# Attention scores by two full 128-row passes in a hybrid SSD / differential attention / HGRN2 trunk

## The chip, the cores and the metric

One core of a Trainium2 chip runs the whole kernel. The metric is the device time of one execution in microseconds (us). TensorE (PE, with its weight loads shown apart as PEld), VectorE (DVE), ScalarE (ACT), GpSimd (POOL) and SyncE (SP) each work through their own list of instructions in order and wait for one another by semaphores. DMAs are issued from the SP, ACT and POOL queues.

## What is computed

Two residual layers on 1024 tokens of 1024 channels, then an RMSNorm. The part at issue is the differential attention of layer 0: 8 heads, each with two softmax maps of 64 channels.

```python
s = jnp.einsum("bqhcd,bkhcd->bhcqk", qi, k).astype(jnp.float32) * scale + bias[None, :, None]
s = jnp.where(rel >= 0, s, -jnp.inf)
p = jax.nn.softmax(s, axis=-1)
w = p[:, :, 0] - lam * p[:, :, 1]
return jnp.einsum("bhqk,bkhv->bqhv", w.astype(v.dtype), v)
```

The index c is the map (2), d the 64 channels of a map. Queries are taken in 8 row tiles of 128 tokens; row tile i needs (i + 1) * 128 keys.

## The kernel before

All products are made from float32r operands. Where more precision is wanted, an operand is held as a high part (its rounding) and a low part (the rest), and a product is the sum of high x high, high x low and low x high. Weights come in blocks of 256 columns (`_wprep`, L100 to L119: DMA, cast on ACT at L116, subtraction on DVE at L117), projections with channels on the partitions are made by `mm_cm` (L158, 24 passes of 512 tokens into one PSUM bank `pj`), those with tokens on the partitions by `mm_tm` (L168, passes of 256 columns).

Layer 0 does the four SSD groups first and then, for each of the 8 attention heads, `att_qk` (projects q and k of both maps), in most heads a projection of values or gates, and `att_core`. In `att_core`, `soft(i)` makes the scores of row tile i for map 0 and map 1 (L545, into one of the two `big` banks each), adds the bias and takes the row maximum (DVE L549, L553), exponentiates (ACT L559) and combines the maps (DVE L566). `values(i)` transposes the weights (PE L577, ACT L579) and multiplies them by V (PE L581). `norm` and its `tail` finish four row tiles (POOL L132, PE L600, DVE L627).

`att_qk` makes five tiles of 128 partitions x 1024 tokens per head, all from the pool tag "A" with 11 slots. Two are q's, one per map m: the 64 rows of the map hold the high part of q / 8, the other 64 its low part. `kh` holds the high parts of k of both maps below each other (ACT L519). Two are `kbs`: k's low part on the rows of the map (DVE L521) and k's high part on the other rows, which a DMA from the POOL queue brings from `kh` (L524, 64 rows x 1024, twice per head). A score is then a sum of two passes: q (128 rows) with `kbs` (128 rows), which gives both mixed products, and q's high rows with `kh`'s rows of that map (64 rows), which gives high x high.

The order of instructions on each engine is set by the Tile scheduler, which moves work of the next head and its projections between the steps of the present one; a slot of a pool is reused when its last reader is done, and what is to be written there waits for that reader.

Of the kernel before, what the change touches and what calls it, by code (L numbers as in the profile page):

```python
# [10 lines left out]
F32 = mybir.dt.float32  # L11
F32R = mybir.dt.float32r
# [21 lines left out]
def host_consts():  # L34
    c = {}
    c["ident"] = np.eye(P, dtype=np.float32)
    c["triu"] = np.triu(np.ones((P, P), np.float32))
    m = np.arange(384)
    rel = 255 - m
    n = np.maximum(rel, 0)  # L40
    large = 16 + (np.log(np.maximum(n, 1).astype(np.float32) / np.float32(16))
                  / np.float32(math.log(8.0)) * np.float32(16)).astype(np.int32)
    bucket = np.where(n < 16, n, np.minimum(large, 31))
    oh = np.zeros((33, 384), np.float32)
    oh[bucket, m] = (rel >= 0).astype(np.float32)
    oh[32] = np.where(rel < 0, NEG, 0.0)
    c["onehot"] = oh
    # HGRN2: keys (rows, modulo 32) that a query column of a region takes its weight from
    s = (np.arange(P) % 32)[:, None]
    reg = []  # L50
    for h, lo, hi in ((1, 0, 1), (2, 0, 2), (4, 2, 4), (4, 0, 2), (8, 0, 8), (16, 8, 16), (16, 0, 8)):
        seg, j = np.meshgrid(np.arange(16 // h), np.arange(h), indexing="ij")
        t = (seg * 2 * h + h + j).reshape(1, -1)
        o = s % (2 * h)
        reg.append(np.tile((s // (2 * h) == t // (2 * h)) & (o >= lo) & (o < hi), (1, NT)))
    c["lvmask"] = np.concatenate(reg, axis=1).astype(np.float32)
    c["dgmask"] = np.tile(s == np.arange(32)[None, :], (1, NT)).astype(np.float32)
    return c


SLOTS = {  # tag: (bytes per partition, slots); tiles of all phases share them
# [12 lines left out]
class Net:  # L74
# [22 lines left out]
    # weights: 256-column blocks, split exactly into two float32r parts  # L97
# [40 lines left out]
    # one 128-channel tile of u^T for four token tiles, times the norm's weight, split  # L138
# [10 lines left out]
    # channel-major product: [128 channels, 512 tokens]  # L149
# [12 lines left out]
    # token-major product: [128 tokens, 256 channels]  # L162
# [8 lines left out]
    # values, token-major, for two heads: two tiles of four token tiles  # L171
# [15 lines left out]
    # 2 silu(channel-major product), two tiles of 128 channels  # L187
# [21 lines left out]
def setup_rows(S):  # L209
# [5 lines left out]
    # per-channel vectors: rows of 128, turned into columns  # L215
# [29 lines left out]
def setup_rest(S):  # L245
# [10 lines left out]
    # HGRN2 lower bound of layer 1: softmax over the layers, its running sum less the first  # L256
# [21 lines left out]
    # lambda of the differential attention, on every partition  # L278
# [13 lines left out]
    # position bias: far value per head; near values in every row, read back skewed as Toeplitz tiles  # L292
# [15 lines left out]
def softplus(S, out, x, ax, e, s, s2):  # L308
    """max(x,0) + log1p(exp(-|x|)), log1p(e) = 2 atanh(e / (2 + e))"""
# [16 lines left out]
def dt_stage(S, u):  # L326
    """dt and the running sums of dt * A, tokens on the partitions: [128, chunk, head]"""
# [90 lines left out]
def ssd_core(S, g, xs, Bt, Ct, zg, ya):  # L418
# [4 lines left out]
    for c in range(NT):  # L423
# [44 lines left out]
        if c % 2 == 1:  # L468
            c2 = slice((c - 1) * P, (c + 1) * P)
            # exp(a_cs) along the rows, two heads per block  # L470
# [26 lines left out]
def att_qk(S, u):  # L497
    """q / 8 and k in two float32r parts: per map q's stacked, k's stacked the other way round (the mixed
    products in one pass), and both maps' high parts of k below each other"""
    nc = S.nc  # L500
    w = S.wnext()
    rows = slice(0, 64), slice(64, 128)
    qs = [S.t("A", [P, L], F32R) for _ in range(2)]
    for hf in range(2):
        sl = slice(hf * 512, hf * 512 + 512)
        pj = S.ps("pj")
        S.mm_cm(pj, w, 0, u, hf)
        for m in range(2):
            q, src = qs[m], pj[rows[m]]
            nc.scalar.activation(q[rows[m], sl], src, AF.Copy, scale=0.125)  # L510
            nc.vector.scalar_tensor_tensor(q[rows[1 - m], sl], src, 0.125, q[rows[m], sl].bitcast(F32),
                                           op0=ALU.mult, op1=ALU.subtract)
    kh = S.t("A", [P, L], F32R)
    kbs = [S.t("A", [P, L], F32R) for _ in range(2)]
    for hf in range(2):
        sl = slice(hf * 512, hf * 512 + 512)
        pj = S.ps("pj")
        S.mm_cm(pj, w, 1, u, hf)
        nc.scalar.copy(kh[:, sl], pj)  # L519
        for m in range(2):  # L520
            nc.vector.tensor_tensor(kbs[m][rows[m], sl], pj[rows[m]], kh[rows[m], sl].bitcast(F32),  # L521
                                    op=ALU.subtract)
    for m in range(2):
        nc.gpsimd.dma_start(kbs[m][rows[1 - m]], kh[rows[m]])  # L524
    return [(qs[m], kbs[m], qs[m][rows[m]], kh[rows[m]]) for m in range(2)]


def att_core(S, h, qk, V, sg, yb, tail):
    """tail: the last rows of the head before; returns its own"""
# [4 lines left out]
    def soft(i):  # L534
# [3 lines left out]
        for m in range(2):  # L538
            s = S.ps("big")
            f = max(n - 256, 0)  # L540
            for k0 in range(0, n, 512):
                kn = min(512, n - k0)
                for j in range(2):
                    q, k = qk[m][2 * j:2 * j + 2]
                    nc.tensor.matmul(s[:, k0:k0 + kn], lhsT=q[:, isl], rhs=k[:, k0:k0 + kn],  # L545
                                     start=(j == 0), stop=(j == 1))
# [76 lines left out]
def emit_y(S, pt, wcol, gate, dst):  # L623
    """(o^T * w) * gate for 512 tokens, stored"""
    nc = S.nc
    y = S.t("ey", [P, 512])
    nc.vector.scalar_tensor_tensor(y, pt, wcol, gate, op0=ALU.mult, op1=ALU.mult)  # L627
    nc.sync.dma_start(dst, y)


def load_y(S, y_d, wcols, hf, k, tags):
    """channel tiles k, k + 1, ... of y^T for 512 tokens, split: [hi | lo]"""
# [19 lines left out]
def out_proj(S, y_d, wcols, x_d, x1_tags, rs_a, finish):  # L652
    """x + y @ w_out in two parts: the channels that are there early for all tokens, which fills the wait
    for the others, then the others for 512 tokens at a time; finish(half, x1, 1 / rms)"""
# [41 lines left out]
    for hf in range(2):  # L696
        started = hf == 0
        if started:
            # all but the last channels, which come late: one open sum per bank
# [7 lines left out]
        for cb in range(4):  # L707
            # the last sums token tile by token tile, each in a bank of its own
# [61 lines left out]
def norm_first(S, x, wcol):  # L770
    """u of x in DRAM"""
# [54 lines left out]
def layer0(S, x, x1_d, u1):  # L826
# [14 lines left out]
    # 1 / rms of the gated rows (they carry a factor of two)  # L841
# [19 lines left out]
def layer1(S, x1_d, u, out):  # L861
# [50 lines left out]
    def early(cb, x1):  # L912
        # the norm's weight ahead of the row's scale; the squares are read before
        if cb < 3:
            nc.vector.tensor_tensor(x1, x1, bc(fws[cb].unsqueeze(1), list(x1.shape)), op=ALU.mult)
# [19 lines left out]
def hgrn_core(S, hd, g1, f, K, V, g2, att, lvm, dgm, yo):  # L935
    """Pairs (key, query) are split by the smallest block of 2h tokens that holds both; queries carry the
    decay from a boundary between the two, keys the decay up to it. One stationary key variant serves a
    level and the next one, whose queries come twice: for the far keys with the missing decay on top."""
# [69 lines left out]
    # keys of 32 and of 64 tokens; the former's weights on the partitions that the latter leaves  # L1008
# [14 lines left out]
    # the chunk's weights, keys on the partitions  # L1023
# [15 lines left out]
    # states  # L1039
# [80 lines left out]
```

## Time and profile before

| what | value |
|---|---|
| three runs | 2345.0, 2345.65 (median), 2347.86 us |
| profiled execution: span | 2346.1 us, 40804 instructions |
| PE busy | 2262.1 us (96%), 16868 matmuls |
| PEld / DVE / ACT / POOL busy | 1927.1 (82%) / 1269.5 (54%) / 824.8 (35%) / 187.5 us (8%) |
| chain that ended last | PE 83%, DMA 10%, DVE 4%, ACT 2%, issue 1% |
| L545 in it (`big`, the scores) | 5% |
| attention scores | L545, x384, first at 508.6 us, last at 1112.8 us |
| DMA issues of L524 | x16, 256 KB each, 5.5 us median from issue to landing |

The page gives no time for the profiled execution other than its span of 2346.1 us; that is 0.45 us over the median of the three runs. PE is the busy engine, but matmuls are pipelined and the profile models their ends, so the sum of their durations overstates them: the time that a matmul takes from PE is read as the distance from its start to the next one's start. The sentence "issue" behind an idle time means that the engine waited for nothing that the profile shows.

### The profile page before, as it was taken

What the parts mean: (1) busy time and instruction counts of PE and PEld (TensorE: products, weight loads), DVE (VectorE), ACT (ScalarE), POOL (GpSimd) and SP (SyncE); (2) the same over time, 40 slices, a digit from 0 to 9 for tenths busy, and PEclk for the clock granted to TensorE, in tenths of its full rate; (3) what the DMA queues carried; (4) which work ended last, traced back from release to release, by engine and by line L of the source; (5) the groups of instructions that cost most, each with busy time, mean ns of one, the idle gap of its engine ahead of it and who ended that gap; (6) DMA issues with size and microseconds to landing.
All of it is one profiled execution on the core that took longest, in us unless ns stands there. A gap on an engine that the chain in (4) does not pass through costs nothing.

```text
span 2346.1 us, 40804 instructions
## 1 busy us (share of the span) xinstructions
PE 2262.1 (96%) x16868; PEld 1927.1 (82%) x16868; DVE 1269.5 (54%) x2838; ACT 824.8 (35%) x1887; POOL 187.5 (8%) x201
## 2 busy tenths in 40 slices
PE   6959989899999999999999999999999999999998
PEld 4747766788778787788998888888888888989998
DVE  4736657535554545665444355555646465557444
ACT  4413333224444444544343223332323232334233
POOL 1000111100000000000001010101011010100000
PEclk9979999999999999999999999999999999999999
DMA  5342323231211211231432111111111111124323
GB/s 131 63 78 69 94 73 85 60 82 37 50 46 36 50 39 52 82 128 37 156 123 85 37 55 54 47 46 46 46 46 46 46 50 42 55 65 153 123 94 126
DMA packets 180701, 166.29 MB, mean 71 GB/s; under 512 B 9431, under 2 KB 162401, under 8 KB 180516
## 3 DMA queue, kind: packets, MB, share of 16 engines
q1 hardware_dynamic: 173668, 152.42, 21.5%
q0 software_dynamic: 2624, 7.08, 2.0%
q10 hardware_dynamic: 4224, 4.19, 0.5%
q8 instruction: 132, 2.16, 0.4%
q14 instruction: 53, 0.43, 0.1%
HBM read 132.66 MB, written 26.80 MB: 68 GB/s over the span
## 4 chain that ended last, share of the span: by engine, by line
PE 83%; DMA 10%; DVE 4%; ACT 2%; issue 1%; SPq 0%; POOL 0%; ACTq 0%; POOLq 0%; DVEq 0%
PE pj L158 38%; PE pj L168 21%; DMA G<-acs_d 6%; PE big L545 5%; PE big L168 5%; PE s L581 3%; PE big L976 2%; DMA tz_d<-o 1%; PE s L577 1%; PE big L1064 1%; PE big L1066 1%; PE s L1053 1%; DVE G L442 1%; PE big L1018 1%; DVE w_lo L117 1%
## 5 line engine op out<-in xcount | busy, mean ns | idle before, releaser
L158 PE MATMUL pj<-u,w_hi 128*128 128x512 f32 x3072 | 988.4, 399 | 12.2 <-ACT A L397 8.5
L158 PEld LDWEIGHTS pj<-u,w_hi 128*128 128x128 f32 x3072 | 570.4, 189 | 136.5 <-ACT A L397 9.7
L158 PE MATMUL pj<-u,w_lo 128*128 128x512 f32 x1536 | 609.7, 397 | 0.0
L168 PE MATMUL pj<-w_hi,u 128*128 128x256 f32 x2592 | 496.5, 287 | 1.0 <-DVE A L206 1.0
L168 PEld LDWEIGHTS pj<-w_hi,u 128*128 128x128 f32 x2592 | 409.6, 191 | 9.5 <-issue 5.6
L168 PE MATMUL pj<-w_lo,u 128*128 128x256 f32 x1296 | 370.2, 286 | 0.0
L158 PEld LDWEIGHTS pj<-u,w_lo 128*128 128x128 f32 x1536 | 290.2, 189 | 61.4 <-issue 2.2
L117 DVE TENSOR_TENSOR w_lo<-w_raw,w_hi 128x1024 fp32r<-128x1024 f32 x168 | 204.6, 1240 | 104.4 <-ACT w_hi L116 104.2
L168 PEld LDWEIGHTS pj<-w_lo,u 128*128 128x128 f32 x1296 | 248.0, 191 | 1.7 <-issue 0.6
L116 ACT CAST w_hi<-w_raw 128x1024 fp32r<-128x1024 f32 x168 | 168.0, 1046 | 200.2 <-PE pj L158 113.7
L545 PE MATMUL big<-A 128*128 128x512 f32 (+7 forms) x384 | 142.0, 420 | 0.0
L206 DVE SCALAR_TENSOR_TENSOR A<-th,pj 128x512 f32<-128x512 f32 x80 | 55.0, 688 | 143.9 <-ACT th L205 143.3
L205 ACT ACTIVATE th<-pj 128x512 f32<-128x512 f32 x96 | 57.2, 596 | 207.5 <-PE pj L158 202.7
L559 ACT ACTIVATE p<-p,mx 128x256 f32<-128x256 f32 (+7 forms) x128 | 98.7, 772 | 84.2 <-DVE mx L555 76.4
L545 PEld LDWEIGHTS big<-A 128*128 128x128 f32 (+1 forms) x384 | 71.2, 185 | 58.9 <-issue 50.6
L132 POOL TENSOR_TENSOR ro<-rs_t,mhalf 128x4 f32<-128x4 f32 x48 | 53.2, 1109 | 828.3 <-DVE rs_t L131 663.3
L579 ACT COPY wT<-s 128x512 f32<-128x512 f32 (+2 forms) x96 | 45.9, 478 | 134.4 <-PE s L577 133.9
L442 DVE TENSOR_SCALAR G<-G,ph 128x128 f32<-128x128 f32 x128 | 28.9, 287 | 108.1 <-DMA G<-acs_d 108.1
L893 POOL TENSOR_SCALAR A<-th,fN,fB 128x512 f32<-128x512 f32 x32 | 47.6, 1488 | 470.0 <-ACT th L890 470.0
L581 PE MATMUL s<-V,wT 128*128 128x128 f32 x576 | 81.2, 277 | 0.0
L960 DVE TENSOR_TENSOR A<-A,p 128x512 f32<-128x512 f32 x96 | 65.7, 685 | 23.5 <-PE big L976 23.0
L581 PEld LDWEIGHTS s<-V,wT 128*128 128x128 f32 x576 | 73.8, 191 | 4.5 <-issue 1.6
(328 smaller groups left out, 3030.7 us busy)
## 6 DMA issues: line engine op xcount, KB each, us to landing
w_raw<-in_even_w_in SPq DMA_DIRECT2D x32, 512.0 KB, 4.7
w_raw<-in_odd_w_in SPq DMA_DIRECT2D x64, 256.0 KB, 3.5
w_raw<-in_odd_w_in SPq DMA_DIRECT2D x32, 512.0 KB, 3.9
w_raw<-in_even_w_in SPq DMA_DIRECT2D x48, 256.0 KB, 3.9
w_raw<-in_even_w_out SPq DMA_DIRECT2D x24, 512.0 KB, 4.4
w_raw<-in_odd_w_out SPq DMA_DIRECT2D x24, 512.0 KB, 5.2
G<-acs_d SPq DMA_DIRECT2D x32, 256.0 KB, 4.7
yo<-ey SPq DMA_DIRECT2D x32, 256.0 KB, 2.0
```

What stands on the lines that cost most here:

```text
L116: nc.scalar.copy(hq, raw)
L117: nc.vector.tensor_tensor(lq, raw, hq.bitcast(F32), op=ALU.subtract)
L132: nc.gpsimd.tensor_tensor(dst, t[:, :n], self.mhalf[:, :n], op=ALU.pow)
L158: nc.tensor.matmul(out, lhsT=ww[:, k, ms], rhs=uu[k][:, sl], start=(n == 0), stop=(n == 3 * KT - 1))
L168: nc.tensor.matmul(out, lhsT=uu[k], rhs=ww[:, k, :], start=(k == 0 and j == 0), stop=(k == KT - 1 and j == 2))
L205: nc.scalar.activation(th, pj, AF.Tanh, scale=0.5)
L206: nc.vector.scalar_tensor_tensor(out, view(th), 1.0, view(pj), op0=ALU.add, op1=ALU.mult)
L442: nc.vector.tensor_scalar(R[:, h], R[:, h], S.acs[:, c, 4 * g + h:4 * g + h + 1], 0.0, op0=ALU.subtract, op1=ALU.min)
L545: nc.tensor.matmul(s[:, k0:k0 + kn], lhsT=q[:, isl], rhs=k[:, k0:k0 + kn], start=(j == 0), stop=(j == 1))
L559: nc.scalar.activation(p[:, :n], p[:, :n], AF.Exp, bias=mx, accum_out=z)
L581: nc.tensor.matmul(po[:, i % 4, :], lhsT=wT[:, j * P:j * P + P], rhs=V(j, hh), start=(j == 0), stop=(j == i))
L960: nc.vector.tensor_tensor(k, k, bc(halves(Ts[h], 1)[1], [P, L // (2 * h), h]), op=ALU.mult)
```

## The change

`att_qk` now treats k as it treats q: per map one tile `ks` with k's high part on the map's 64 rows (ACT) and its low part on the other 64 (DVE). A second tile per map, `xs`, is `ks` with its two halves exchanged, made by two DMAs of 64 rows x 1024 from the POOL queue. A score is again a sum of two passes, both of 128 rows: q with `ks` (high x high and low x low) and q with `xs` (the two mixed products). The number of passes stays at 384; the product low x low is new. Per head there are six tiles of tag "A" instead of five, four DMAs of 256 KB instead of two, and for each half of k two ACT instructions on 64 rows instead of one on 128.

```diff
-    kh = S.t("A", [P, L], F32R)
-    kbs = [S.t("A", [P, L], F32R) for _ in range(2)]
-    for hf in range(2):
...
-        S.mm_cm(pj, w, 1, u, hf)
-        nc.scalar.copy(kh[:, sl], pj)
-        for m in range(2):
-            nc.vector.tensor_tensor(kbs[m][rows[m], sl], pj[rows[m]], kh[rows[m], sl].bitcast(F32),
-                                    op=ALU.subtract)
+    out = []
+    for mt, scale in ((0, 0.125), (1, 1.0)):
+        ts = [S.t("A", [P, L], F32R) for _ in range(2)]
+        for hf in range(2):
...
+            S.mm_cm(pj, w, mt, u, hf)
+            for m in range(2):
+                t, src = ts[m], pj[rows[m]]
+                nc.scalar.activation(t[rows[m], sl], src, AF.Copy, scale=scale)
+                nc.vector.scalar_tensor_tensor(t[rows[1 - m], sl], src, scale, t[rows[m], sl].bitcast(F32),
+                                               op0=ALU.mult, op1=ALU.subtract)
+        out.append(ts)
+    qs, ks = out
+    xs = [S.t("A", [P, L], F32R) for _ in range(2)]
     for m in range(2):
-        nc.gpsimd.dma_start(kbs[m][rows[1 - m]], kh[rows[m]])
-    return [(qs[m], kbs[m], qs[m][rows[m]], kh[rows[m]]) for m in range(2)]
+        for r in range(2):
+            nc.gpsimd.dma_start(xs[m][rows[r]], ks[m][rows[1 - r]])
+    return [(qs[m], (ks[m], xs[m])) for m in range(2)]
...
+                q, ks = qk[m]
                 for j in range(2):
-                    q, k = qk[m][2 * j:2 * j + 2]
-                    nc.tensor.matmul(s[:, k0:k0 + kn], lhsT=q[:, isl], rhs=k[:, k0:k0 + kn],
+                    nc.tensor.matmul(s[:, k0:k0 + kn], lhsT=q[:, isl], rhs=ks[j][:, k0:k0 + kn],
                                      start=(j == 0), stop=(j == 1))
```

In the changed file the score line is L541, the DMAs are L520, transposes L573, values L577, the tail's transposes L596.

The scheduler also orders the work anew. On PE, before the change, 28 projection passes of L158 stand between the last scores of head 3 (row tile 7, bank `big_6066`) and the first scores of head 4 (`big_6402`, `big_6411`; its q tiles are A_6153 and A_6154). The end of that stretch:

```order
L158 MATMUL pj_6827<-u_81,w_hi_6274 128x512
L158 MATMUL pj_6827<-u_89,w_hi_6274 128x512
L158 MATMUL pj_6827<-u_81,w_lo_6275 128x512
L581 MATMUL s1_5981<-V_4282,wT_6028 128x128 [waits Activation_49]
L581 MATMUL s1_5981<-V_4282,wT_6028 128x128
L600 MATMUL s1_6045<-ident_71,o_5931 128x128 [waits PE_49]
L600 MATMUL s1_6045<-ident_71,o_5931 128x128 x3
L545 MATMUL big_6402<-A_6214,A_6153 128x128 [waits DMASW2_49,DVE_49]
L545 MATMUL big_6402<-A_6213,A_6153 128x128
L545 MATMUL big_6411<-A_6215,A_6154 128x128 [waits DMASW3_49,DVE_49]
L545 MATMUL big_6411<-A_6213,A_6154 128x128
L158 MATMUL pj_6827<-u_82,w_hi_6274 128x512
```

The first pass of each map reads `kbs` and waits for its DMA; the second reads `kh` and does not.

After the change, the same place: ahead of these rows stand the eight passes of row tile 7 of head 3, four for map 0 (`big_6073`) and then four for map 1 (`big_6086`). In the rows, `ks` of head 4 is A_6233 and A_6234, `xs` A_6293 and A_6294.

```order
L573 MATMUL s1_6055<-ident_71,p0_5976 128x128 [waits Activation_49]
L573 MATMUL s1_6055<-ident_71,p0_5976 128x128
L577 MATMUL s1_6001<-V_4191,wT_6048 128x128 x4
L577 MATMUL s1_6001<-V_4292,wT_6048 128x128 [waits Activation_49]
L577 MATMUL s1_6001<-V_4292,wT_6048 128x128
L596 MATMUL s1_6065<-ident_71,o_5951 128x128 [waits PE_49]
L596 MATMUL s1_6065<-ident_71,o_5951 128x128 x3
L541 MATMUL big_6427<-A_6233,A_6173 128x128 [waits DVE_49]
L541 MATMUL big_6427<-A_6293,A_6173 128x128 [waits DMASW3_49,DMASW2_49]
L541 MATMUL big_6436<-A_6234,A_6174 128x128 [waits DVE_49]
L541 MATMUL big_6436<-A_6294,A_6174 128x128 [waits DMASW5_49,DMASW4_49]
```

No projection pass is left between the two heads, and now the second pass of each map waits for DMAs, two of them. Between heads 5 and 6 the rows are the same but for their numbers; at the other five head boundaries 54 to 223 passes stand between the last scores of map 0 and the first pass that reads map 1's `xs`.

On the POOL queue the DMAs of heads 4 and 5 stood like this before (A_6214 and A_6215 are `kbs` of head 4, A_6857 and A_6858 of head 5; `ro` is the row scale of `norm`):

```order
L524 DMA A_6214<-A_6213 64x1024 [waits DMASW7_49,Activation_49]
L524 DMA A_6215<-A_6213 64x1024 [waits DMASW6_49,PE_49]
L132 TENSOR_TENSOR ro_5945<-rs_t_5946,mhalf_69 128x4 [waits DVE_49,Pool_49]
L524 DMA A_6857<-A_6856 64x1024 [waits DMASW1_49,Activation_49]
L524 DMA A_6858<-A_6856 64x1024 [waits DMASW0_49,PE_49]
L132 TENSOR_TENSOR ro_6138<-rs_t_6139,mhalf_69 128x4 [waits DVE_49,Pool_49]
```

They stand like this after (A_6941 is map 0's `xs` of head 5):

```order
L520 DMA A_6293<-A_6233 64x1024 [waits Activation_49]
L520 DMA A_6293<-A_6233 64x1024 [waits DVE_49]
L132 TENSOR_TENSOR ro_5422<-rs_t_5423,mhalf_69 128x4 [waits DVE_49,Pool_49]
L132 TENSOR_TENSOR ro_5965<-rs_t_5966,mhalf_69 128x4 [waits DVE_49,Pool_49]
L520 DMA A_6294<-A_6234 64x1024 [waits DMASW6_49,DMASW4_49,DMASW7_49,PE_49,Activation_49]
L520 DMA A_6294<-A_6234 64x1024 [waits DMASW5_49]
L520 DMA A_6941<-A_6881 64x1024 [waits Activation_49]
L520 DMA A_6941<-A_6881 64x1024 [waits DVE_49]
L132 TENSOR_TENSOR ro_6158<-rs_t_6159,mhalf_69 128x4 [waits DVE_49,Pool_49]
```

The two DMAs of map 1 have moved behind two of `norm`'s row scales and wait for PE: two heads ask for 12 tiles of "A" where there are 11 slots, and the slot of A_6294 is that of A_5557, map 0's `xs` of head 3, which the four passes into `big_6073` read last.

## Rows read from the trace of the kernel before

**Rows 1.** Page, top line and busy time of each engine

```profile
span 2346.1 us, 40804 instructions
PE 2262.1 (96%) x16868; PEld 1927.1 (82%) x16868; DVE 1269.5 (54%) x2838; ACT 824.8 (35%) x1887; POOL 187.5 (8%) x201
```

**Rows 2.** Busy time by stage: stretch, length, engines, granted clock, DMA share, GB/s

```profile
508.00:1115.00 607.00, 607.00 (x3413) 490.42 (x3412) 324.74 (x1009) 262.13 (x646) 24.27 (x30) 1.00 0.20 56
```

**Rows 3.** Chain of waits from 500 to 1115 us, by line

```profile
by line: PE pj L158 40.4%; PE pj L168 23.8%; PE big L545 19.8%; PE s L581 10.1%; PE s L577 4.9%; PE s L600 1.0%
```

**Rows 4.** PE in order of time: start, us, operation; scores 512 wide

```profile
889.21 1.68 PE L545 MATMUL big<-A 128*128 128x512 f32 x4
890.81 0.73 PE L158 MATMUL pj<-u,w_hi 128*128 128x512 f32 x2
891.38 0.39 PE L158 MATMUL pj<-u,w_lo 128*128 128x512 f32 x1
891.61 0.62 PE L158 MATMUL pj<-u,w_hi 128*128 128x512 f32 x2
...
892.31 0.62 PE L158 MATMUL pj<-u,w_hi 128*128 128x512 f32 x2
```

**Rows 5.** Weight loads of the same stretch in order of time

```profile
889.96 0.19 PEld L545 LDWEIGHTS big<-A 128*128 128x128 f32 x1 [0.24 <-issue]
890.39 0.18 PEld L545 LDWEIGHTS big<-A 64*128 64x128 f32 x1 [0.24 <-issue]
```

**Rows 6.** PE in order of time: scores 384 wide, then 128 wide

```profile
605.80 0.70 PE L545 MATMUL big<-A 128*128 128x384 f32 x2
606.43 0.50 PE L158 MATMUL pj<-u,w_hi 128*128 128x512 f32 x1
606.77 0.40 PE L158 MATMUL pj<-u,w_lo 128*128 128x512 f32 x1
...
664.58 0.99 PE L545 MATMUL big<-A 128*128 128x128 f32 x4
665.50 0.72 PE L158 MATMUL pj<-u,w_hi 128*128 128x512 f32 x2
666.06 0.39 PE L158 MATMUL pj<-u,w_lo 128*128 128x512 f32 x1
```

**Rows 7.** PE in order of time: passes 256 wide, then values 128 wide

```profile
739.07 0.28 PE L168 MATMUL pj<-w_lo,u 128*128 128x256 f32 x1
...
739.91 0.28 PE L168 MATMUL pj<-w_hi,u 128*128 128x256 f32 x1
...
748.46 1.06 PE L581 MATMUL s<-V,wT 128*128 128x128 f32 x8
749.27 0.48 PE L158 MATMUL pj<-u,w_lo 128*128 128x512 f32 x1
```

**Rows 8.** DMA issues of L524: ns min/median/max of one; landing

```profile
L524 POOL DMA_DIRECT2D A<-A x16: 517/526/602, 467.9 to 989.8; - x16
...
DMA to landing us min/median/max: 2.9/5.5/7.8
```

**Rows 9.** Busy time around an idle time of PE, columns as in rows 2

```profile
402.00:405.00 3.00, 0.82 (x5) 0.36 (x3) 2.18 (x2) 3.00 (x5) 1.40 (x2) 1.00 0.00 0
405.00:410.00 5.00, 5.00 (x15) 3.98 (x16) 5.00 (x6) 1.33 (x2) 0.00 (x0) 0.66 0.71 210
```

**Rows 10.** Instructions of k's and q's evictions: ns min/median/max of one

```profile
L519 ACT CAST A<-pj x16: 574/586/592, 454.2 to 988.4; 128x512 fp32r<-128x512 f32 x16
L521 DVE TENSOR_TENSOR A<-pj,A x32: 673/688/696, 457.8 to 989.8; 64x512 fp32r<-64x512 f32 x32
L510 ACT ACTIVATE A<-pj x32: 582/592/595, 429.8 to 972.2; 64x512 fp32r<-64x512 f32 x32
L511 DVE SCALAR_TENSOR_TENSOR A<-pj,A x32: 683/685/694, 434.9 to 973.6; 64x512 fp32r<-64x512 f32 x32
```

More of the change, by code (lines that the diff above doesn't have):

```diff
@@ L502, in att_qk @@
     rows = slice(0, 64), slice(64, 128)
-    qs = [S.t("A", [P, L], F32R) for _ in range(2)]
-    for hf in range(2):
-        sl = slice(hf * 512, hf * 512 + 512)
-        pj = S.ps("pj")
-        S.mm_cm(pj, w, 0, u, hf)
-        for m in range(2):
[L509 to L512, printed above, removed]
-    kh = S.t("A", [P, L], F32R)
-    kbs = [S.t("A", [P, L], F32R) for _ in range(2)]
-    for hf in range(2):
-        sl = slice(hf * 512, hf * 512 + 512)
-        pj = S.ps("pj")
-        S.mm_cm(pj, w, 1, u, hf)
-        nc.scalar.copy(kh[:, sl], pj)
-        for m in range(2):
-            nc.vector.tensor_tensor(kbs[m][rows[m], sl], pj[rows[m]], kh[rows[m], sl].bitcast(F32),
-                                    op=ALU.subtract)
+    out = []
+    for mt, scale in ((0, 0.125), (1, 1.0)):
+        ts = [S.t("A", [P, L], F32R) for _ in range(2)]
+        for hf in range(2):
+            sl = slice(hf * 512, hf * 512 + 512)
+            pj = S.ps("pj")
+            S.mm_cm(pj, w, mt, u, hf)
[7 more added lines that the diff above has]
+    xs = [S.t("A", [P, L], F32R) for _ in range(2)]
     for m in range(2):
-        nc.gpsimd.dma_start(kbs[m][rows[1 - m]], kh[rows[m]])
-    return [(qs[m], kbs[m], qs[m][rows[m]], kh[rows[m]]) for m in range(2)]
+        for r in range(2):
+            nc.gpsimd.dma_start(xs[m][rows[r]], ks[m][rows[1 - r]])
+    return [(qs[m], (ks[m], xs[m])) for m in range(2)]
 def att_core(S, h, qk, V, sg, yb, tail):
```

## Prediction

> **What bounds the kernel now.** I read the page first: PE is busy for 2262 of 2346 us and every other engine for at most 54% [rows 1]. That is an average, so the next view is the stage that the change touches, 508 to 1115 us, where the eight heads run: there PE is busy for all 607.00 us, at a granted clock of 1.00 (2.4 GHz), with VectorE at 325 and ScalarE at 262 us [rows 2]. The chain of waits over this stretch consists of PE alone, its shares adding up to 100%, and the scores hold 19.8% of it [rows 3]. So in this stage a microsecond taken from PE's list is a microsecond of the kernel, as long as nothing makes PE wait. What a pass takes is then read as the distance between starts in PE's order of time.
>
> **What a 64-row pass costs.** An L158 pass of 512 columns takes 0.23 us (891.38 to 891.61; three passes from 891.61 to 892.31 take 0.70) [rows 4]. Scores of the same width take longer: from 889.21 to 891.38 run four of them (128, 64, 128, 64 rows) and two L158 passes, 2.17 us, where six at 0.23 would take 1.38. The loss is 0.79 us for two 64-row passes, 0.40 each. The weight loads tell why: each one at a change of rows starts only when the load unit has stood idle for 0.24 us, and takes 0.18 to 0.19 us in full view [rows 5], so that neighbouring loads are 0.43 us apart. The first L158 pass behind the scores also pays: 0.57 us for two passes (890.81 to 891.38) instead of 0.46.
>
> The loss hardly depends on the width down to 256. At 384 columns two scores and one L158 pass take 0.97 us (605.80 to 606.77) [rows 6]; at full speed the two would take 0.175 each (an estimate midway between 0.12 for 256 columns, seven passes in 0.84 us [rows 7], and 0.23 for 512), 0.58 in all: 0.39 lost on one 64-row pass. At 128 columns four scores and two L158 passes take 1.48 us (664.58 to 666.06) [rows 6]; at full speed a 128-column pass takes about 0.11 (eight value passes in 0.81 us, and 0.12 for the wider ones [rows 7]), so 0.90 in all: 0.29 lost per 64-row pass. For 256 columns I take 0.39.
>
> **The change, part by part.** *Scores.* All 384 passes have 128 rows afterwards, and no change of rows is left. Per head and map the eight row tiles hold 12 passes of 512 columns and 4 each of 384, 256 and 128, half of them of 64 rows. Over 16 pairs of head and map that is 96 of 512 columns at 0.40, 32 of 384 and 32 of 256 at 0.39, 32 of 128 at 0.29: 38.4 + 25.0 + 9.3 = **72.7 us saved**. The number of passes stays, and the added product low x low is inside the first one, so no column is added.
>
> *Waits for `xs`.* PE now needs two DMAs where one `kbs` was needed, and at heads 4 and 6 they cannot start early: they wait for a slot that the last scores of the head before release. Behind that release PE has 19 passes ahead of the one that waits, 4 scores of 512 columns and 15 passes of 128: 4 x 0.23 + 15 x 0.11 = 2.6 us. Of the DMAs, the first issue takes 0.53 us on POOL and the second lands 5.5 us after its own issue, 2.9 at the least and 7.8 at the most [rows 8]: 6.0 us (3.4 to 8.4) after the release. PE stands for 3.4 us (0.8 to 5.8) twice: **7 us lost**, between 2 and 12. A smaller wait would be there anyway, since the banks of `big` are read by VectorE first. Everything behind it on PE waits too, and no later slack gives it back, because PE is the bound. At the other boundaries 54 or more passes stand between; with mostly 0.12 and 0.23 us each that is over 8 us, about what the slowest landing needs: nothing taken.
>
> By the Trainium skill (DMA: Bandwidth & Descriptors, Anatomy of one DMA) a DMA from GpSimd takes 2.0 us plus its bytes at 436 GB/s, an estimate of 2.6 us for 256 KB; the two waits would then be 1 us together and the sum 2274. The trace has a median of 5.5 us for this very DMA, and I go by that.
>
> *Clock.* After 2.2 us in which PE stood (402 to 405 us) the granted clock of the next 5 us was 0.66, a mixture of 2.4 and 1.2 GHz [rows 9]; at full work that costs 5 x 0.34 = 1.7 us. Two stalls may pay this twice or not at all: 0 to 3.4, I take **1.7 us lost**.
>
> *Evictions of k.* ScalarE gets two copies of 64 rows (0.59 us) for one of 128 rows (0.59), 16 more in all, 9.4 us; VectorE's two keep their length (0.685 against 0.688) [rows 10]. ScalarE is busy for 262 of 607 us, and the projection bank is released after the second VectorE instruction as before, so this costs nothing while a projection of 24 passes (5.5 us) runs in the other bank. Without that cover it would be those 9.4 us.
>
> *POOL and its queue.* 16 more issues of 0.53 us are 8.5 us on an engine that is busy for 24 of 607 [rows 2, 8]. Behind the waiting DMAs stand map 0's `xs` of the next head and head 3's second row scale; the one waits for projections that PE reaches only after the stall, the other for values that come later still. Nobody waits for them: 0. The row scales that now stand ahead of the DMA belong to values made long before: 0. On SP's queue no step is added; one load of x into "A" moves some places back, since its slot comes free later, and its reader is the sum of an output block that PE reaches only after another block's 192 passes of 0.12 us, 23 us: 0.
>
> *Cover.* PE's stretch shrinks to some 540 us, where VectorE's 325 are 60% and ScalarE's 272 are 50%; the softmax chains keep their length, and PE reaches their results up to 1.6 us earlier per row tile. I put that at 0 and give it a rival.
>
> The sum against the profiled execution: 2346.1 - 72.7 + 7 + 1.7 = 2282.1. Its span lies 0.45 us over the median of the runs, so I predict **2282 us**, 2.7% less.
>
> **Rivals.** *A, less gain: PE waits at more places.* The landing of 256 KB beside weight loads reaches 7.8 us [rows 8]; if it comes to 4 us more than I take, heads 4 and 6 cost 8 more and four other boundaries 2 to 3 each; a softmax result that comes late at a tenth of the 64 row tiles by 1 us costs 6. Together 10 to 30 us: 2292 to 2312. For it: two DMAs per map in place of one, and a slot too few. Against it: before, PE never stood in 607 us [rows 2].
>
> *B, slower: the row count is not what spaces the passes.* If the 0.43 us came from something that stays, such as two passes reading the same q tile as weights, the gain is nil and the two waits with their clock remain: 2346 + 9 = 2355. It decides where less than 9 / 192 = 0.05 us is saved per 64-row pass. Against it: L158 passes also add into one bank one after another and take 0.23, and the excess stands at each change of rows, also in the L158 pass behind the scores [rows 4, 5].
>
> *C, slower: the 64-row passes are cheap.* If the two maps' 64-row passes ran side by side, on rows 0 to 63 and 64 to 127, 96 of them would be free now; the change would then pay up to 96 x 0.2 = 19 us for them and 9 for the waits: 2374. The Trainium skill (TensorE: Matmul & The Clock Gate, section Why this matters for your kernels) says that small-K passes on separate row groups run concurrently. The trace shows them one after another, with a 128-row pass between [rows 4, 5].
>
> *D, more gain: the DMAs land before PE needs them.* With 2.6 us or less after the release nothing is lost: 2346 - 73 = 2273. For it speaks only the shortest landing, 2.9 us [rows 8], which still leaves 0.8.
>
> **How the numbers follow.** My forecast (2274 to 2291, one to six us per wait, prices of a 64-row pass within 5%) has 0.65, A 0.22, D 0.08, B 0.03 and C 0.01; 0.01 is for a gain that the waits just cancel. The range for 8 in 10 takes in the forecast, D's end and most of A: 2271 to 2304. A measurement of this kernel tells some 0.2% (4.7 us) from no change. Faster: 0.65 + 0.22 + 0.08 = 0.95; same 0.01; slower 0.04.
>
> **What would show it.** In the changed profile a stretch of four score passes of 512 columns behind L158 should take about 0.92 us from its first start to the next operation, not 1.60; no 64-row weight load should be left, and the attention stage should last some 545 us. PE should have two idle times of 1 to 6 us at the starts of heads 4 and 6, ended by a DMA into "A" from POOL, with a fall of the clock behind one or both. I am wrong if the distance of scores stays near 0.43, or if PE's idle time in the stage adds up to over 20 us.

## The result, and the profile after

Over four runs each, the changed kernel took **2288.12 us** (median; 2285.82 to 2289.96) against 2345.32 us (2343.26 to 2347.86) for the kernel before on the same chip: ratio 0.9751, 95% interval 0.9737 to 0.9765. That is 57 us less. In two further sets of runs, below, the ratio was 0.9741 and 0.9739. The span of the profiled execution fell from 2346.1 to 2284.9 us, by 61.2 us.

The page of the changed kernel, top and busy times, answers to [rows 1]:

```profile
span 2284.9 us, 40859 instructions
PE 2195.1 (96%) x16868; PEld 1923.2 (84%) x16868; DVE 1270.9 (56%) x2838; ACT 832.8 (36%) x1903; POOL 197.9 (9%) x217
```

PE makes as many matmuls as before in 67 us less of busy time. The first score pass now stands at 477.5 us and not at 508.6, the last at 1047.9 and not at 1112.8: the scheduler starts the scores earlier, so that the length of the stage cannot be held against the 545 us that the prediction gave for it. The window over the stage, with the columns of [rows 2]:

```profile
484.00:1050.00 566.00, 560.05 (x3531) 503.90 (x3530) 327.49 (x1014) 273.43 (x667) 34.47 (x47) 0.99 0.25 68
```

PE is still nearly always busy, but no longer quite: 5.95 us of idle time, and a granted clock of 0.99. The chain of waits over this stretch, by line, answers to [rows 3]:

```profile
by line: PE pj L158 41.6%; PE pj L168 22.7%; PE big L541 10.9%; PE s L577 8.9%; PE s L573 4.6%; DMA w_raw<-ya 1.6%; DVE p L549 1.3%; issue 1.1%; DVE A L513 0.9%; PE s L596 0.9%; DMA w_raw<-in_even_w_out 0.8%; ACT p L555 0.7%; DVE u L639 0.7
```

The scores went from 19.8% of 615 us to 10.9% of 565, from 122 to 62 us, and VectorE's rows (L549, L513) have come into a chain that was PE alone.

PE in order of time, scores 512 columns wide behind L158, as in [rows 4]:

```profile
848.67 0.63 PE L158 MATMUL pj<-u,w_hi 128*128 128x512 f32 x2
849.13 1.07 PE L541 MATMUL big<-A 128*128 128x512 f32 x4
850.04 0.39 PE L158 MATMUL pj<-u,w_lo 128*128 128x512 f32 x1
850.27 0.61 PE L158 MATMUL pj<-u,w_hi 128*128 128x512 f32 x2
```

Four scores take 0.91 us (849.13 to 850.04), and the L158 pass behind them takes its usual 0.23. The 64-row weight loads of [rows 5] are gone: in the view that keeps forms apart, where 192 of the kernel before's weight loads for scores have 128 rows and 192 have 64, all 384 now have 128:

```profile
L541 PEld LDWEIGHTS big<-A 128*128 128x128 f32 x384 | 64.3, 189 | 14.3 <-DVE mf L549 5.3 <-issue 1.0
```

If the distances from each score's start to PE's next start are added up over the whole trace, they make 134.2 us before and 73.0 after (the four passes behind which PE stopped are counted at 0.11 us, like others of 128 columns). The pass of another line behind a group of scores takes some 0.10 us less in 105 places, 11 us. Together **72 us**.

What PE lost again stands at the starts of heads 4 and 6. PE in order of time at the first of them (an idle time ahead of a row, and what ended it, in brackets):

```profile
788.54 1.50 PE L577 MATMUL s<-V,wT 128*128 128x128 f32 x12
789.88 0.60 PE L596 MATMUL s<-ident,o 128*128 128x128 f32 x4
791.15 0.44 PE L541 MATMUL big<-A 128*128 128x128 f32 x2 [0.67 <-DVE mf L549]
793.21 0.44 PE L541 MATMUL big<-A 128*128 128x128 f32 x2 [1.62 <-DVE mf L549]
793.87 0.66 PE L573 MATMUL s<-ident,p 128*128 128x128 f32 x4 [0.23 <-DVE ey L623]
794.60 0.75 PE L158 MATMUL pj<-u,w_hi 128*128 128x512 f32 x2
```

The idle times add up to 2.52 us, and to 2.52 again at 928 us: 5.0 in all. None of them is ended by a DMA. The rows of VectorE say what it was doing:

```profile
787.88 1.15 DVE L562 SCALAR_TENSOR_TENSOR p<-p,rr,p 128x896 f32<-128x896 f32 x1
789.07 0.69 DVE L513 SCALAR_TENSOR_TENSOR A<-pj,A 64x512 fp32r<-64x512 f32 x1
...
790.13 0.95 DVE L549 CUSTOM_DVE_ANT_0 p<-big,far 128x768 f32<-128x768 f32 x1
...
791.12 0.69 DVE L513 SCALAR_TENSOR_TENSOR A<-pj,A 64x512 fp32r<-64x512 f32 x1
...
792.19 0.95 DVE L549 CUSTOM_DVE_ANT_0 p<-big,far 128x768 f32<-128x768 f32 x1
793.07 0.08 DVE L549 DVE_READ_ACCUMULATOR2_ANT mf<- 128x1 f32 x1
793.07 0.75 DVE L623 SCALAR_TENSOR_TENSOR ey<-s,subw,G 128x512 f32<-128x512 f32 x1
793.85 0.69 DVE L513 SCALAR_TENSOR_TENSOR A<-pj,A 64x512 fp32r<-64x512 f32 x1
```

VectorE still reads the last score banks of head 3 (L549, done at 791.09 and 793.15, 0.06 us ahead of the two PE rows), and between them it evicts q of head 5 (L513). PE has no other work in its list there: the next projection pass stands behind these rows and starts at 794.60, 0.06 us after an L513 row has ended. Map 1's `xs`, for which the prediction had PE wait, was issued by POOL as two DMAs at 787.86 and 788.44:

```profile
L520 POOL DMA_DIRECT2D A<-A x2: 517/545/573, 787.9 to 788.4; - x2
...
DMA to landing us min/median/max: 3.0/3.3/3.6
```

They landed 2.97 and 3.64 us later, the last at 792.1, before map 1's bank was free (793.15). The DMA was hidden and not early: the last pass ahead of head 4's scores ends at 790.48 (789.88 + 0.60), and PE would have come to the first pass that reads this `xs` near 790.7, an estimate from these rows. With free banks the DMA would have held it for some 1.4 us.

Behind both stops the clock fell to a mixture of 2.4 and 1.2 GHz, as behind the stop of [rows 9]:

```profile
795.00:800.00 5.00, 5.00 (x17) 3.95 (x16) 2.56 (x6) 2.47 (x5) 0.00 (x0) 0.66 0.09 32
930.00:935.00 5.00, 4.45 (x14) 3.41 (x15) 2.96 (x9) 2.96 (x5) 0.19 (x1) 0.67 0.21 79
```

That is 1.7 us each, 3.4 in all.

### The profile page after: what moved, and what is told of

The parts are those of the page before. It is cut to its first block, busy times and chain, and to the rows that moved or that the text cites. A ratio compares the mean times of both kernels' runs of the same rounds, so it can differ in the third digit from the quotient of the medians.

```text
span 2284.9 us, 40859 instructions
## 1 busy us (share of the span) xinstructions
PE 2195.1 (96%) x16868; PEld 1923.2 (84%) x16868; DVE 1270.9 (56%) x2838; ACT 832.8 (36%) x1903; POOL 197.9 (9%) x217
## 4 chain that ended last, share of the span: by engine, by line
PE 79%; DMA 11%; DVE 6%; ACT 2%; issue 1%; SPq 0%; POOL 0%; ACTq 0%; POOLq 0%; DVEq 0%
PE pj L158 38%; PE pj L168 20%; DMA G<-acs_d 6%; PE big L168 5%; PE big L541 3%; PE s L577 2%; PE big L972 2%; DMA tz_d<-o 1%; PE big L1060 1%; PE s L573 1%; PE big L1062 1%; PE s L1049 1%; DVE G L442 1%; ACT w_hi L116 1%; PE big L1014 1%
## 5 line engine op out<-in xcount | busy, mean ns | idle before, releaser
L158 PE MATMUL pj<-u,w_hi 128*128 128x512 f32 x3072 | 987.8, 399 | 11.5 <-ACT A L397 7.8
L158 PEld LDWEIGHTS pj<-u,w_hi 128*128 128x128 f32 x3072 | 572.5, 190 | 131.6 <-ACT A L397 9.1
L158 PE MATMUL pj<-u,w_lo 128*128 128x512 f32 x1536 | 609.2, 397 | 0.0
L168 PE MATMUL pj<-w_hi,u 128*128 128x256 f32 x2592 | 495.6, 287 | 1.2 <-DVE A L206 1.0
L168 PEld LDWEIGHTS pj<-w_hi,u 128*128 128x128 f32 x2592 | 412.2, 192 | 4.5 <-DVE A L206 1.4
L168 PE MATMUL pj<-w_lo,u 128*128 128x256 f32 x1296 | 369.9, 285 | 0.0
L158 PEld LDWEIGHTS pj<-u,w_lo 128*128 128x128 f32 x1536 | 291.2, 190 | 60.3 <-issue 0.9
L168 PEld LDWEIGHTS pj<-w_lo,u 128*128 128x128 f32 x1296 | 249.2, 192 | 0.9
L541 PE MATMUL big<-A 128*128 128x512 f32 (+3 forms) x384 | 90.3, 352 | 5.2 <-DVE mf L549 5.2
L577 PE MATMUL s<-V,wT 128*128 128x128 f32 x576 | 79.6, 275 | 0.0
L956 DVE TENSOR_TENSOR A<-A,p 128x512 f32<-128x512 f32 x96 | 65.8, 686 | 23.5 <-PE big L972 23.0
L577 PEld LDWEIGHTS s<-V,wT 128*128 128x128 f32 x576 | 74.2, 191 | 2.7 <-ACT wT L575 0.4
L541 PEld LDWEIGHTS big<-A 128*128 128x128 f32 x384 | 64.3, 189 | 14.3 <-DVE mf L549 5.3
```

Of the source, the lines that this page charges most:

```text
L158: nc.tensor.matmul(out, lhsT=ww[:, k, ms], rhs=uu[k][:, sl], start=(n == 0), stop=(n == 3 * KT - 1))
L168: nc.tensor.matmul(out, lhsT=uu[k], rhs=ww[:, k, :], start=(k == 0 and j == 0), stop=(k == KT - 1 and j == 2))
L541: nc.tensor.matmul(s[:, k0:k0 + kn], lhsT=q[:, isl], rhs=ks[j][:, k0:k0 + kn], start=(j == 0), stop=(j == 1))
L577: nc.tensor.matmul(po[:, i % 4, :], lhsT=wT[:, j * P:j * P + P], rhs=V(j, hh), start=(j == 0), stop=(j == i))
L956: nc.vector.tensor_tensor(k, k, bc(halves(Ts[h], 1)[1], [P, L // (2 * h), h]), op=ALU.mult)
```

## The experiments

Two questions were put to the chip: whether it is the change of rows that costs, the number of 64-row passes, or neither; and what ends the stops at heads 4 and 6. Differences between kernels of different sets of runs are taken from their ratios to the kernel before, with 0.974 to 0.975 for the changed kernel and 1% = 23.5 us. A group is a run of 64-row passes without another form between; how many there are was counted in each trace.

**One pass back to 64 rows.**

```diff
-                for j in range(2):
-                    nc.tensor.matmul(s[:, k0:k0 + kn], lhsT=q[:, isl], rhs=ks[j][:, k0:k0 + kn], ...)
+                own = slice(64 * m, 64 * m + 64)
+                nc.tensor.matmul(s[:, k0:k0 + kn], lhsT=q[:, isl], rhs=ks[1][:, k0:k0 + kn], ...)
+                nc.tensor.matmul(s[:, k0:k0 + kn], lhsT=q[own, isl], rhs=ks[0][own, k0:k0 + kn], ...)
```

> The changed kernel with one thing undone: the pass that makes high x high reads only the map's own 64 rows of q and ks, after the pass with xs; evictions, DMAs, slots and the order of the work stay. Theory 1 (each 64-row pass among 128-row ones costs 0.40, 0.39 or 0.29 us): all 72.7 us come back on PE, 2288 + 73 = 2361 (2355 to 2364), above the kernel before, because the two stops at the starts of heads 4 and 6 stay. Rival (the gain came from the new order, or from the layout of q and k): 2288 (2284 to 2294).

Measured: 2353.07 us, ratio 1.0025 (1.0015 to 1.0035), some 66 us over the changed kernel and 0.25% slower than the kernel before. So the new layout, the DMAs and the order of the work gain nothing by themselves; the row count of one pass carries the gain. PE in order of time, four 512-wide scores and what follows:

```profile
889.23 0.39 PE L541 MATMUL big<-A 128*128 128x512 f32 x1
889.55 0.50 PE L543 MATMUL big<-A 64*128 64x512 f32 x1
889.97 0.49 PE L541 MATMUL big<-A 128*128 128x512 f32 x1
890.40 0.50 PE L543 MATMUL big<-A 64*128 64x512 f32 x1
890.83 0.38 PE L168 MATMUL pj<-w_hi,u 128*128 128x256 f32 x1
891.05 0.63 PE L158 MATMUL pj<-u,w_hi 128*128 128x512 f32 x2
```

The distance of 0.43 us of the kernel before is back. The rows also say how a change is paid: the pass ahead of it takes 0.32 (889.23 to 889.55) and not 0.23, the pass behind it 0.1 more as well (the L168 row 0.22 and not 0.12). A change of rows costs 0.19 to 0.2 us at these widths, half on either side, and a 64-row pass between 128-row ones has two; by the 0.29 us of 128-column scores [rows 6] it is some 0.15 there. The sum missed by some 7 us; 2.3 of these are that the stops were 1.37 us each and not 2.5.

**The same passes, fewer changes of rows.** The j loop goes outside the k0 loop:

```diff
-            for k0 in range(0, n, 512):
-                kn = min(512, n - k0)
-                q, ks = qk[m]
-                for j in range(2):
+            q, ks = qk[m]
+            own = slice(64 * m, 64 * m + 64)
+            for j, rw in ((1, slice(0, P)), (0, own)):
+                for k0 in range(0, n, 512):
+                    kn = min(512, n - k0)
```

> As the run with 64 rows, but of each score tile first all 128-row passes (xs) and then all 64-row passes: of 192 places where a 64-row pass stands between 128-row passes 128 are left; the number of 64-row passes is the same. Theory 1a (the price is one of the change of rows): 16 x (0.29 + 0.39 + 0.39 + 0.40) = 23.5 us less than the run with 64 rows, some 2337. Theory 1b (each 64-row pass is slow by itself): the same time as that run, some 2361.

Measured: 2327.2 us, ratio 0.9914 (0.9895 to 0.9934), 26 us less than with the passes in turn, where 23.5 were expected from 64 groups fewer. The trace has 128 groups in place of 192. Four 512-wide scores, 128, 128, 64 and 64 rows:

```profile
876.99 1.28 PE L542 MATMUL big<-A 128*128 128x512 f32 x4
878.21 0.39 PE L168 MATMUL pj<-w_hi,u 128*128 128x256 f32 x1
878.43 0.62 PE L158 MATMUL pj<-u,w_hi 128*128 128x512 f32 x2
```

They take 1.22 us, with one group, where the run above takes 1.60 with two. Theory 1a holds and 1b falls: the price belongs to the change, and not to the 64-row pass.

**All passes on 64 rows.** The same loop as the changed kernel, with `own` in both operands and j in (1, 0).

> Leaves out q low x k high: both passes of a score read the map's own 64 rows (xs, then ks), so no 128-row pass stands inside a score tile; DMAs and slots stay. Theory 1a (change of rows): one price per score tile, at most 128 x 0.38 = 49 us over the changed kernel, 2337, and 24 over it, 2312, where the two maps stand next to each other. Theory 1b (each 64-row pass slow by itself): 384 x 0.38 = 145 us over it, 2433.

Measured: 2310.12 us, ratio 0.9832 (0.9812 to 0.9851), 20 us over the changed kernel. With 1b it would have been 2433. It is also less than 1a gives: the trace has 102 groups, 39 us at 0.38. The rows show why. Where the scheduler left the two maps next to each other, four 512-wide passes (two per map, in turn):

```profile
538.78 0.74 PE L542 MATMUL big<-A 64*128 64x512 f32 x4
539.44 0.50 PE L158 MATMUL pj<-u,w_lo 128*128 128x512 f32 x1
...
563.86 1.18 PE L542 MATMUL big<-A 64*128 64x512 f32 x4
564.97 0.39 PE L168 MATMUL pj<-w_hi,u 128*128 128x256 f32 x1
```

take 0.66 us (first two rows); four of one map take 1.11 (last two). The passes of map 0 read rows 0 to 63, those of map 1 rows 64 to 127, and they write into different banks: in the first group the passes of a pair start 7 and 9 ns apart and run **side by side**. The four of one map, on the same rows, start 0.23 us or more apart, also where the columns that they write change from the first 512 to the next; passes on different rows into one bank were not tried. There are 84 pairs that start less than 45 ns apart, and each saves the time of one pass, together 15 us (40 of 512 columns at 0.23, 10 of 384 at 0.17, 19 of 256 at 0.12, 15 of 128 at 0.11): 39 - 15 = 24, near the 20 measured.

**The two maps' 64-row passes next to each other.**

```diff
+        ss = [S.ps("big") for _ in range(2)]
+        for j in (1, 0):
+            for k0 in range(0, n, 512):
+                kn = min(512, n - k0)
+                for m in range(2):
+                    q, ks = qk[m]
+                    rw = slice(64 * m, 64 * m + 64) if j == 0 else slice(0, P)
+                    nc.tensor.matmul(ss[m][:, k0:k0 + kn], lhsT=q[rw, isl], rhs=ks[j][rw, k0:k0 + kn], ...)
```

> The 128-row passes of both maps first, then the 64-row passes, map 0 (rows 0 to 63) and map 1 (rows 64 to 127) in turn, into different banks: one group of 64-row passes per row tile, 64 in all. If passes on different rows run side by side: the 64-row passes, 34.8 us in all at full speed (16 x (6 x 0.228 + 2 x 0.172 + 2 x 0.12 + 2 x 0.11)), cost half, 17 us less than the changed kernel, and 64 groups x 0.40 = 26 more: 2297. If one after another: 2288 + 26 = 2314. To either some us come on top where PE waits for both banks at once; the distance between starts in PE's order of time decides: two 512-wide 64-row passes in 0.23 us or in 0.46.

Measured: 2318.34 us, ratio 0.9866 (0.9847 to 0.9886). The total lies near the second value, but for another reason: the scheduler did not keep the maps together. The trace has 111 groups and not 64, and only 29 pairs side by side: 111 x 0.38 = 42 us, less 5 for the pairs, is 37 over the changed kernel; measured are 28. Of the 9 between, 5 are that its stops at heads 4 and 6 are 1.48 us each and draw no fall of the clock. Where a pair stands together, the weight loads show it:

```profile
768.66 0.19 PEld L541 LDWEIGHTS big<-A 64*128 64x128 f32 x2 [0.35 <-issue]
769.10 0.19 PEld L158 LDWEIGHTS pj<-u,w_hi 128*128 128x128 f32 x1 [0.25 <-issue]
```

Two 64-row loads in the 0.19 us of one. The Trainium skill (TensorEngine Tiling (Array Packing), Tiling Modes, Key Properties) says that tiles of one mode load and multiply in parallel, and that a change of mode drains TensorE. Both runs agree: pairs start together, and each change costs some 0.2 us.

**What ends the stops.** Three runs in one set, with the changed kernel beside them.

> The changed kernel once more, as the measure for the three runs on the same chip: 0.9751 of the kernel before, some 2288 us.

Measured: 2285.6 us, ratio 0.9741 (0.9726 to 0.9755).

First, without the DMAs that wait for a slot:

```diff
-    xs = [S.t("A", [P, L], F32R) for _ in range(2)]
-    for m in range(2):
+    nx = 1 if h in (4, 6) else 2
+    xs = [S.t("A", [P, L], F32R) for _ in range(nx)] + ks[nx:]
+    for m in range(nx):
```

> In heads 4 and 6 map 1 has no xs: its second pass reads ks again (the two mixed products of map 1 are left out there, high x high and low x low counted twice). So 11 slots are enough, and the DMAs that waited for a slot are gone; the order of PE's work stays. Theory of the prediction (the late DMAs of map 1 stop PE at the starts of heads 4 and 6): the stops of 2.5 us go with half or all of the clock's price, 2288 - 5 to 8 = 2280 to 2283. Rival (VectorE, which reads the score banks between evictions of the next q, ends the stops): 2288 (2286 to 2290), both stops still about 2.5 us.

Measured: 2285.87 us, ratio 0.974 (0.9727 to 0.9753), no difference. PE in order of time at the start of head 4:

```profile
791.22 0.44 PE L542 MATMUL big<-A 128*128 128x128 f32 x2 [0.68 <-DVE mf L550]
793.27 0.44 PE L542 MATMUL big<-A 128*128 128x128 f32 x2 [1.62 <-DVE mf L550]
793.94 0.66 PE L574 MATMUL s<-ident,p 128*128 128x128 f32 x4 [0.23 <-DVE ey L624]
```

Without the DMAs the two waits for VectorE's L550 are the same to 0.01 us (0.67 and 1.62 us at head 6 too). That these DMAs stop PE is refuted.

Second, with less for VectorE to do there:

```diff
+                if mt == 0 and h in (5, 7):
+                    nc.scalar.activation(t[rows[1 - m], sl], src, AF.Copy, scale=scale)
+                    continue
```

> In heads 5 and 7 the low rows of q get its high part, copied by ScalarE, in place of the difference that VectorE makes (q low x k is left out there, as a right product): VectorE has 8 evictions of 0.69 us less, ScalarE 8 of 0.59 us more; DMAs and slots stay. VectorE theory: the stops at the starts of heads 4 and 6 fall from 2.5 to under 1 us each and the clock stays up, 2288 - 3 - 3 = 2282 (2279 to 2284). DMA theory of the prediction: they stay or grow, 2288 (2286 to 2291).

Measured: 2284.87 us, ratio 0.9741 (0.9726 to 0.9755), no difference in the total. The stop at head 4 fell from 2.52 to 0.64 us (ended by ScalarE), and at head 6, 0.31 us of idle time is left in the 20 us from 920; but a new one stands at the start of head 5, again ended by VectorE:

```profile
858.21 0.42 PE L544 MATMUL big<-A 128*128 128x128 f32 x2 [0.60 <-DVE rr L562]
861.91 0.80 PE L158 MATMUL pj<-u,w_hi 128*128 128x512 f32 x1 [2.09 <-DVE A L516]
```

The expectation on the place was right, that on the time wrong: the scheduler had moved the projections, and the stop moved with them. Near 1110 us, where the layers meet, this trace also has 1.1 us more of idle time and 1.7 us more of slow clock than that of the changed kernel.

Third, with q's low part made by GpSimd from a copy in SBUF, in all heads (the diff is that of the last run, without `h >= 4`):

> Computes the same as the changed kernel. In all heads q's projection bank is emptied by one ScalarE copy of 128 rows into SBUF (0.6 us); the high part is copied from there by ScalarE and the low part is made by GpSimd, not by VectorE: 32 evictions of 0.69 us = 22 us less on VectorE, 16 copies more on ScalarE, 32 subtractions on GpSimd. The scheduler then leaves 26 projection passes between heads 3 and 4 and between 5 and 6, about 6 us of cover. VectorE theory: both stops of 2.5 us and their slow clock (3.4 us) go: 2288 - 8 = 2280 (2278 to 2284). Rival (the stops come back elsewhere, as ScalarE or GpSimd is late): 2288 (2285 to 2292).

Measured: 2289.74 us, ratio 0.9768 (0.9752 to 0.9784), slower than the changed kernel. The stops at heads 4 and 6 went, but the tail of the SSD stage grew worse. The window from 430 to 484 us of this kernel:

```profile
430.00:484.00 54.00, 39.66 (x187) 28.33 (x187) 29.51 (x82) 13.93 (x26) 15.67 (x18) 0.75 0.25 64
```

The changed kernel has 46.77 us of PE, 279 matmuls and a clock of 0.94 in the same window. The copy of q takes its place from the tag "th", which the SSD stage's squares use too; that this held back head 0's projections, which fill PE there, is the likely reason, but it was not separated from GpSimd's own time. Both belong to head 0: with head 0 left to VectorE, in the next set, PE has 46.93 us and 273 matmuls in this window.

**The same in fewer heads.** Three kernels in another set of runs.

> The changed kernel again, as the measure for the two runs on the same chip: 0.9741 to 0.9751 of the kernel before, 2285 to 2288 us.

> Computes the same as the changed kernel: as the run with q's low part on GpSimd, but from head 1 on; head 0 keeps VectorE, so that no GpSimd subtraction of 1.33 us stands between the last SSD steps. If that run lost its gain to GpSimd in the SSD tail (PE's stops of 2.41 to 4.55 us there), the stops at heads 4 and 6 stay away and those of the SSD tail shrink to those of the changed kernel: 5 us of stops and 3.4 of slow clock less than the changed kernel on this chip, 0.9963 of it (0.995 to 0.998). If GpSimd and ScalarE are late elsewhere too: 0.999 to 1.002 of it.

> Computes the same as the changed kernel: q's low part on GpSimd in heads 4 to 7 alone, where the scheduler again leaves 26 projection passes at the starts of heads 4 and 6. The same 0.9963 of the changed kernel, if only these two places matter (0.995 to 0.998); if the gain of the run from head 1 on has another source, less than that run's.

```diff
+            if mt == 0 and h >= 4:
+                st = S.t("th", [P, 512])
+                nc.scalar.activation(st, pj, AF.Copy, scale=scale)
+                for m in range(2):
+                    t = ts[m]
+                    nc.scalar.copy(t[rows[m], sl], st[rows[m]])
+                    nc.gpsimd.tensor_tensor(t[rows[1 - m], sl], st[rows[m]], t[rows[m], sl].bitcast(F32),
+                                            op=ALU.subtract)
+                continue
```

Measured: the changed kernel 2285.24 us (ratio 0.9739, 0.9725 to 0.9752); from head 1 on 2281.83 us (0.9727, 0.9713 to 0.974); from head 4 on **2281.12 us** (0.9715, 0.9701 to 0.9728). The last was run once more.

> The run with q's low part on GpSimd in heads 4 to 7 once more, to see whether its gain over the changed kernel stands: again 0.971 to 0.973 of the kernel before (the changed kernel had 0.9741 and 0.9739); if the gain was chance, 0.974 or more.

Measured: 2280.97 us, ratio 0.9728 (0.9715 to 0.9741). Two runs near 0.972 stand against three near 0.9745: some 4 to 5 us better than the changed kernel, with intervals that overlap in part. The windows around heads 4 and 6, from head 4 on:

```profile
780.00:800.00 20.00, 20.00 (x109) 17.12 (x107) 10.08 (x31) 11.36 (x28) 6.73 (x7) 1.00 0.15 34
920.00:940.00 20.00, 20.00 (x115) 17.19 (x114) 12.26 (x33) 13.44 (x24) 6.72 (x7) 1.00 0.24 70
```

and of the changed kernel:

```profile
780.00:800.00 20.00, 17.41 (x88) 14.25 (x87) 13.22 (x34) 8.18 (x16) 2.10 (x3) 0.91 0.18 47
920.00:940.00 20.00, 17.41 (x93) 14.44 (x92) 13.07 (x39) 9.09 (x20) 1.66 (x3) 0.91 0.17 46
```

PE is busy throughout at full clock. In each window 2.59 us of idle time have gone and 1.8 us of slow clock (20 x 0.09), 8.8 us in all, of which about half arrives at the end. In its two traces PE stands 1.2 and 1.7 us longer near 1110 us than in that of the changed kernel; the rest of the other half was not traced. Nor was it separated whether the shorter hold on the projection bank (one copy) or VectorE's lighter load is what lets the scheduler put projections there.

## Why the prediction was right, point by point

The time, 2288.12 us where 2282 were forecast, lies in the range, and the main mechanism is shown. Not every step held: the wait at heads 4 and 6 came from another engine than the prediction said, and that its size came out near is luck.

- **PE bounds the stage: right.** 72 us less on PE's list became 61 us less in the span, and 64 rows in one pass took 66 us back.
- **The price of a 64-row pass, 72.7 us: right, and right in its place.** The direct sum is 72. Four scores take 0.91 us, 0.92 were expected. That it stands at the change of rows is shown by the run with grouped passes: the price goes with the changes, not with the passes, and all-64-row scores run at full speed inside a group. That the weight load in full view is what takes the time at a change, as the prediction has it, fits its 0.18 to 0.19 us [rows 5], but no run separated it from anything else that a change may need.
- **The waits for `xs`, 7 us: the size nearly right (5.0), the releaser wrong.** The prediction took 5.5 us, the median of all L524 DMAs [rows 8], as the landing of the second DMA; these landed in 2.97 and 3.64. The step that failed is "PE stands for 3.4 us (0.8 to 5.8) twice" because of the DMAs. It set aside what it calls a "smaller wait", "since the banks of `big` are read by VectorE first"; that was the whole wait, 2.5 us, and it hid the some 1.4 us that the DMAs would have cost. The run without these DMAs has the same two waits for VectorE. The Trainium skill's rule that was weighed (DMA: Bandwidth & Descriptors, Anatomy of one DMA), an estimate of 2.6 us, came nearer to these two landings than the median did, and yet gave the wrong sum, because the wait did not hang on them.
- **The clock, 1.7 us: the mechanism right, the size half.** Both stops drew a fall in the profiled execution, 3.4 us; in the second repetition of the changed kernel only one fall of 1.7 us stood in the heads. The length of the stop alone does not tell: behind the two stops of 1.37 us of the run with one pass back to 64 rows the clock fell both times (0.66 from 830 to 835 us, 0.79 from 985 to 990), behind the two of 1.48 us of the run with the maps next to each other it did not.
- **Evictions, POOL's queue, cover, 0 each: no stop of PE's longer than 0.5 us stands anywhere else in the heads.** But VectorE's "60%" hid that for 10 us around 790 it was busy for over 80% and PE waited for it.
- **The profiled execution against the median: right, but for a reason that it did not give.** A run's time lies 1.8 us over its span (2286.72 against 2284.9 for the changed kernel), so the span of 2346.1 belongs to the slowest of the three runs, 2347.86, which is 2.2 us over the median; the 0.45 is what is left of the two. Of the 6 us between 2282 and 2288.12, 2.8 are in the span (2284.9 against 2282.1), where the second fall of the clock takes 1.7 and smaller differences of either sign were not all traced. The rest is scatter: the profiled execution before lay 2.2 us over its median, the one after 1.4 us under its own. In the two other sets the medians differ by 61.0 and 61.9 us, where the prediction took off 64.
- **Rivals.** A (more waits at other places) did not come. B (the row count is not what spaces the passes) is refuted by the run with one pass back to 64 rows. C (64-row passes side by side) was right about the chip and wrong about this kernel: such passes do run side by side when they are next to each other, and in the kernel before a 128-row pass stood between all 192 of them. D (the DMAs land before PE needs them) did not come true: it asked for 2.6 us or less after the release, and the last one landed 4.2 us after the first was issued (787.86 to 792.1). That was in time only because the banks were later still. Once VectorE is out of the way such a DMA can end a stop: in the second run with GpSimd from head 4 on, PE waits 0.75 us at 992.6 us for a DMA into "A" that took 9.5 us to land.

## What to carry to other kernels

Read what a pass takes as the distance of starts, next to passes of other forms: a pass with fewer rows that is alone among full ones cost 0.4 us here on top of its own 0.23, and filling it up with a useless product was cheaper. If short passes are needed, put them together, and those on different rows and into different banks next to each other (different rows into one bank were not tried). Before naming a DMA as the coming wait, list everything else that the waiting matmul needs, the PSUM bank and its reader's queue above all, and read that engine's load in the 10 us around the place, not over the stage.

## What the runs showed of the hardware that was not expected

A change in the number of columns costs about what a change of rows does. In layer 1 of the changed kernel, 32-column passes (L972) stand among full ones; PE in order of time:

```profile
1203.99 0.40 PE L158 MATMUL pj<-u,w_hi 128*128 128x512 f32 x1
1204.32 0.37 PE L972 MATMUL big<-A 128*32 128x48 f32 x14
1204.62 0.66 PE L143 MATMUL s<-ident,G 128*128 128x128 f32 x4
```

The L158 pass ahead of the change takes 0.33 us and not 0.23; over the 43 places where L972 follows L158 the median is 0.318, and over the 47 where L158 follows L972 it is 0.337. The trace has 709 changes of form before and 325 after: 384 fewer, two for each of the 192 passes, and 384 x 0.19 = 73 us is the gain. Some 190 of those left lie in layer 1; whether they can be saved was not tried.

The 14 passes of L972 in this row take 0.30 us to the start of the next row, 21 ns each, and most of them start 6 or 7 ns behind the one before; the two passes of the 64-row pairs above start 7 and 9 ns apart: PE starts several small passes at once where they leave each other's rows or columns alone.
